# Attention of layer 1: row sums joined on VectorE, maxima spread by one product, and a fixed order on GpSimd

## The chip, the cores and the metric

The kernel runs on one core of one Trainium2 chip. The metric is the device time of one execution, in microseconds. Three executions were timed, and the median counts. One more execution was recorded by the profiler, and every duration of a single instruction below comes from that one.

## What is computed

The reference is a two-layer transformer in float32 over 1024 latent tokens and 256 context tokens of width 1024. Layer 1 mixes tokens by grouped-query attention: 16 query heads share 4 key and value heads of width 64, and each query sees all 1280 keys. Cut to this part it is

```
q = rms_norm(q, q_g); k = rms_norm(k, k_g); q, k = rope(q), rope(k)   # k of the context without rope
s = einsum('bqhgd,bkhd->bhgqk', q, k) * 64 ** -0.5                    # keys: 1024 latent, 256 context
p = softmax(s, axis=-1)
y = einsum('bhgqk,bkhd->bqhgd', p, v) @ w_out
h = h + gate * rms_norm(y, g_post)
```

A gated MLP with a width-3 convolution follows in both layers. The kernel computes its up and down projections by Strassen-like products of halves, for which sums and differences of blocks of the down projection's weights are made ahead of time.

## The kernel before

The attention of layer 1 is `odd_attn`. It walks over 32 blocks; a block is 128 queries of one key head, so four query heads and a tile of 128 x 512 scores per group of 128 keys. Ten such groups of keys make up the 1280. One block goes through these steps, each a small function:

- `maxima` (L1619), once per head: three TensorE products (L1622) give the scores of 128 queries against all 1280 keys in a tile of three PSUM banks, and VectorE takes the negated maximum of each row (L1623). The pool has one such tile, so the products of one head wait until the reduction of the head before has read it.
- `rounded` (L1625) and `shift` (L1629): ScalarE rounds the four columns of negated maxima to the fp32r format (L1627). Then four TensorE products of 128 columns each (L1633), every one with a broadcast column against the identity, turn these columns into rows that are the same on all partitions. ScalarE copies them (L1634) into the second operand of the scores, so that the score product subtracts the maximum by itself.
- `scores` (L1636), once per group of keys: two products of 512 columns (L1642) and an exponential on ScalarE (L1643) into `pT`.
- `values` (L1649): the products of the weights with the values (L1654), in two calls of five groups of keys.
- `first` (L1662) and `second` (L1669): the row sums. GpSimd adds the first eight tiles of `pT` into `part`, seven additions of 128 x 512 (L1667). VectorE adds the last two into `acc` (L1671).
- `sums` (L1656): TensorE multiplies a matrix of ones with `part` and then with `acc` (L1659), in the same PSUM accumulation, which gives the sums over all keys.
- `result` (L1673): VectorE takes the reciprocal (L1675) and multiplies (L1677), and two transfers store the block (L1680).

The blocks overlap. Iteration `n` of the loop holds the scores of block `n`, the second half of the values and `second` of block `n-1`, the sums and the result of block `n-2`, and the maxima of blocks `n+1` and `n+2`. The context manager `in_order` (L1683) keeps TensorE, VectorE and ScalarE in the order in which this loop is written. GpSimd is not listed there: its order, and that of the SyncE queue which issues the transfers, is chosen by the scheduler of the framework from a model of time, as everything outside such a bracket is.

Alongside runs `down_sums` (L609), a generator that prepares the weight sums of the down projection. For each of 11 slices it issues two loads (L618), gives way, makes two subtractions on GpSimd (L613), gives way, makes two more, gives way, issues the store (L628) and gives way. It has one buffer, so the next load waits for the store. The attention loop calls it by `self.steps(ts, 1 + n % 2)` (L1705) at the head of each iteration, one step in even and two in odd iterations. Layer 0 runs a generator of the same kind for its own weights, one step at a time from several loops, without a fixed order on GpSimd.

In iterations 29 to 32 the loop also loads the finished attention of the first 512 tokens and splits it into two operands for the output projection (`out_load`, L1742): ScalarE makes one half and GpSimd the other (L120). The output projection (products L317 to L319) starts right after the loop.

Of the kernel before, what the change touches and what calls it, by code (L numbers as in the profile page):

```python
# [10 lines left out]
F32R = mybir.dt.float32r  # L11
AF = mybir.ActivationFunctionType
ALU = mybir.AluOpType
# [4 lines left out]
P = 128  # L18
# [37 lines left out]
class Net:  # L56
# [92 lines left out]
    def constants(self):  # L149
        nc, a = self.nc, self.a  # L150
        c = lambda shape, tag, dt=F32: self.t(self.cst, shape, tag, None, dt)
        ld = nc.scalar.dma_start
        cv = c([P, KD, 2], "cv")
        ld(cv, a["c_cols"])
        self.ident = c([P, P], "ident")
        ld(self.ident, a["k_ident"])
        self.identr = c([P, P], "identr", F32R)
        nc.vector.tensor_copy(self.identr, self.ident)
        self.mhalf = c([P, 16], "mhalf")
        nc.vector.memset(self.mhalf, -0.5)  # L160
        self.ones = c([P, 64], "ones")
        nc.vector.memset(self.ones, 1.0)
        self.mone = c([P, 1], "mone")
        nc.vector.memset(self.mone, -1.0)
        self.cs = c([P, KD, 32], "cs")
        nc.vector.memset(self.cs, 0.0)
        nc.scalar.activation(self.cs[:, :, 0:2], cv, AF.Silu)
        self.bada = c([P, 2, 48], "bada")
        self.gateD = {}
        self.ada = [c([P, 48, 2], f"ada{l}") for l in range(2)]  # L170
        ld(self.bada, a["b_ada_cols"])
        self.ng = c([P, 2, 4, KD], "ng")
        ld(self.ng, a["norm_g_cols"])
        self.sel = c([P, 2], "sel")
        nc.vector.tensor_tensor(self.sel, self.ident[:, 0:2], self.ident[:, 32:34], op=ALU.add)
        for g in (2, 3):
            nc.vector.tensor_tensor(self.sel, self.sel, self.ident[:, 32 * g:32 * g + 2], op=ALU.add)
# [431 lines left out]
    def down_sums(self, l, pool):  # L609

        nc, w = self.nc, self.a["w_down"][l]
        self.tD[l] = [self.t(self.dr, [P, 2, D], f"tD{l}_{k}") for k in range(NH // 2)]
        sub = lambda o, x, y: nc.gpsimd.tensor_tensor(o, x, y, op=ALU.subtract)  # L613
        for k in range(NH // 2):
            r = self.t(pool(), [P, 2, D], "ts", 1)
            for h in range(2):
                i = k + h * (NH // 2)
                self.tc.keep_in_program_order(nc.sync.dma_start(r[:, h], w[i * P:(i + 1) * P, :]))  # L618
            yield

            (x, y), (u, v) = ((r[:, h, :HF], r[:, h, HF:]) for h in range(2))
            sub(y, y, x)
            sub(v, v, y)
            yield
            sub(x, v, x)
            sub(u, v, u)
            yield
            self.tc.keep_in_program_order(nc.sync.dma_start(self.tD[l][k], r))  # L628
            yield

# [970 lines left out]
    def odd_attn(self, es):  # L1601
        nc, tc = self.nc, self.tc
        with tc.tile_pool(name="ga", reuse_waits="tile", bufs=2) as gp, self.banks(two=1, turn=3, out=2):
            blocks = [dict(p=p, g=g, q=q) for p in range(4) for g in range(4) for q in range(2)]
# [14 lines left out]
            def maxima(b, h):  # L1619
                ps = self.t(self.b2, [P, 1536], "b2")  # L1620
                for c, w in ((0, 512), (512, 512), (T, C)):
                    nc.tensor.matmul(ps[:, c:c + w], b["q1"][:, h], self.KV[b["g"]][0][:, c:c + w], start=True, stop=True)  # L1622
                nc.vector.tensor_reduce(b["ng"][:, h:h + 1], ps[:, :S], axis=AX.X, op=ALU.max, negate=True)  # L1623

            def rounded(b):  # L1625
                b["mr"] = self.t(gp, [P, 4], "mr", 2, F32R)
                nc.scalar.copy(b["mr"], b["ng"])  # L1627

            def shift(b):  # L1629

                ps = self.t(self.bt, [P, 512], "b1")
                for h in range(4):
                    nc.tensor.matmul(ps[:, h * P:(h + 1) * P], b["mr"][:, h:h + 1].to_broadcast([P, P]), self.identr, start=True, stop=True)  # L1633
                nc.scalar.copy(b["q2"][64:P], ps[64:P].rearrange("p (h q) -> p h q", h=4))  # L1634

            def scores(b, k):  # L1636
# [9 lines left out]
            two = lambda x, i: x.rearrange("p (a b q) -> p a b q", a=2, b=2)[:, :, i]  # L1646
            out = lambda x, i: x[i * 64:i * 64 + 64].rearrange("p (a q) -> p a q", a=2)

            def values(b, k0, k1):  # L1649
                if k0 == 0:  # L1650
                    b["po"] = self.t(self.by, [P, 512], "by")
                for k in range(k0, k1):
                    for i in range(2):
                        nc.tensor.matmul(out(b["po"][:, :256], i), self.KV[b["g"]][2][:, k], two(b["pT"][:, k], i), start=(k == 0), stop=(k == NT - 1))  # L1654

            def sums(b):  # L1656
                for x in (b["part"], b["acc"]):
                    for i in range(2):
                        nc.tensor.matmul(out(b["po"][:, 256:], i), self.ones, two(x, i), start=(x is b["part"]), stop=(x is b["acc"]))  # L1659


            def first(b, k0, k1):  # L1662
                if k0 == 0:
                    b["part"] = self.t(gp, [P, 512], "part", 3)
                x = b["part"]
                for k in range(max(1, k0), k1):
                    nc.gpsimd.tensor_tensor(x, x if k > 1 else b["pT"][:, 0], b["pT"][:, k], op=ALU.add)  # L1667

            def second(b):  # L1669
                b["acc"] = self.t(gp, [P, 512], "acc", 3)  # L1670
                nc.vector.tensor_tensor(b["acc"], b["pT"][:, NT - 2], b["pT"][:, NT - 1], op=ALU.add)  # L1671

            def result(b):  # L1673
                rb = self.t(gp, [P, 256], "rb", 2)
                nc.vector.reciprocal(rb, b["po"][:, 256:])  # L1675
                ya = self.t(gp, [P, 256], "ya", 4)
                nc.vector.tensor_tensor(ya, b["po"][:, :256], rb, op=ALU.mult)  # L1677
                c0 = (2 * b["p"] + b["q"]) * P
                for i in range(2):
                    nc.sync.dma_start(self.yT1[2 * b["g"] + i][:, c0:c0 + P], ya[:, i * P:(i + 1) * P])  # L1680

            pinned = ExitStack()
            pinned.enter_context(self.in_order(nc.tensor, nc.vector, nc.scalar))  # L1683
            xp, ts = None, self.down_sums(1, lambda: gp)
            begin(blocks[0])
            begin(blocks[1])
            self.load_keys(gp, 2)
            for h in range(4):
                maxima(blocks[0], h)
            rounded(blocks[0])  # L1690
            for h in range(2):
                maxima(blocks[1], h)
            shift(blocks[0])
            for n in range(len(blocks) + 2):
                b, b1, b2, last, last2 = was(n), was(n + 1), was(n + 2), was(n - 1), was(n - 2)
                if n == 0:
                    self.load_keys(gp, 3)
                if b2:
                    begin(b2)
                if n == 29:  # L1700

                    self.es_g.close()
                    xp = es.enter_context(tc.tile_pool(name="xq", reuse_waits="tile", bufs=1, side="right"))
                    xm = self.xm_tiles(xp)
                self.steps(ts, 1 + n % 2)  # L1705
                if b:
                    scores(b, 0)
                if last2:
                    sums(last2)
                if last:  # L1710
                    values(last, 5, NT)
                if last2:
                    result(last2)
                if b1:
                    maxima(b1, 2)
                if b:
                    for k in (1, 2, 3, 4):
                        scores(b, k)
                    first(b, 0, 5)
                if b1:  # L1720
                    maxima(b1, 3)
                if b:
                    scores(b, 5)
                if b1:
                    rounded(b1)
                if last:
                    second(last)
                if b:
                    values(b, 0, 5)
                if b1:  # L1730
                    shift(b1)
                if b2:
                    maxima(b2, 0)
                if b:
                    for k in (6, 7, 8, 9):
                        scores(b, k)
                    first(b, 5, NT - 2)
                if b2:
                    maxima(b2, 1)
                if 29 <= n < 33:  # L1740
                    for k in (2 * (n - 29), 2 * (n - 29) + 1):
                        self.out_load(xm, k, self.yT1, 0, HF, self.t(gp, [P, 512], "raw", 2), "sp")  # L1742
# [104 lines left out]
```

## Time and profile before

| what | value |
|---|---|
| median of three executions | 2987.95 us |
| lowest and highest | 2986.34 and 2994.62 us |
| profiled execution, its own time | 2988.05 us |
| span of that execution | 2986.3 us |
| mean granted TensorE clock | 0.981 |
| TensorE busy | 2860.5 us, 96% |
| VectorE busy | 2082.2 us, 70% |
| GpSimd busy | 1595.6 us, 53% |
| ScalarE busy | 1295.4 us, 43% |

In the rows further down PE is TensorE's products, PEld its weight loads, DVE is VectorE, ACT is ScalarE, POOL is GpSimd and SP is SyncE. A number such as L1654 is a line of the kernel. A timeline row gives the start and the length in us, the engine, the line, the operation with its output and input tiles, and how many instructions were merged into the row; in square brackets stands the idle time before it and what ended that. A row of groups gives the shapes, the count, the busy time in us, the mean ns of one and the idle time before them.

### The profile page before, as it was taken

Reading aid. Unit: us, or ns where it says so; the run is one execution under the profiler, and the core shown is the slowest. Engines: PE = TensorE matmul, PEld = TensorE weight load, DVE = VectorE, ACT = ScalarE, POOL = GpSimd, SP = SyncE. Lnnn points to the kernel's source line nnn. Section 1 sums busy time; section 2 is a strip of 40 time slices with the busy share of each in tenths; the row PEclk is TensorE's granted clock in tenths of the full one; section 3 lists DMA queues with packets and bytes.
Section 4 is the critical chain, followed back from the end, with each engine's and each line's share of the span. In section 5 each row is a group of like instructions: output and inputs, shape, how many; then the busy total and the mean of one; then the engine's idle time right before and its main releaser. Section 6 shows DMA issues by size and latency. Waiting matters only on the chain.

```text
span 2986.3 us, 43134 instructions
## 1 busy us (share of the span) xinstructions
PE 2860.5 (96%) x15923; PEld 2280.3 (76%) x15923; DVE 2082.2 (70%) x2565; ACT 1295.4 (43%) x2255; POOL 1595.6 (53%) x1500
## 2 busy tenths in 40 slices
PE   8999999998999999999989989999998999999997
PEld 6868877776888888877769966666676788887785
DVE  4441255569776676788987666666647988887998
ACT  4221166473333333444466544444445344444443
POOL 2232268346333333265666778888855644442767
PEclk9999999999999999999999989999999999999999
DMA  9376664552323323543154553323252222225442
GB/s 319 112 239 203 216 238 154 187 185 94 111 91 125 120 97 120 195 162 127 57 188 122 153 165 109 105 90 99 73 175 85 80 86 82 81 82 193 163 141 85
DMA packets 234163, 411.29 MB, mean 138 GB/s; under 512 B 28240, under 2 KB 132688, under 8 KB 226016
## 3 DMA queue, kind: packets, MB, share of 16 engines
q1 hardware_dynamic: 211248, 392.99, 39.1%
q10 hardware_dynamic: 22704, 15.55, 1.7%
q8 instruction: 125, 2.05, 0.3%
q14 instruction: 86, 0.70, 0.1%
HBM read 303.54 MB, written 104.92 MB: 137 GB/s over the span
## 4 chain that ended last, share of the span: by engine, by line
PE 72%; DVE 10%; POOL 6%; DMA 4%; issue 4%; ACT 3%; ACTq 1%; SPq 0%; DVEq 0%; POOLq 0%
PE by L498 8%; PE by L500 8%; PE by L499 8%; PE b L1642 5%; PE by L1654 5%; PE b L1622 3%; PE by L873 3%; PE by L871 3%; PE by L872 3%; PE b L310 2%; PE b L306 2%; PE b L308 2%; DVE wlo L122 2%; PE by L318 2%; PE by L319 2%
## 5 line engine op out<-in xcount | busy, mean ns | idle before, releaser
L461 POOL TENSOR_TENSOR sw<-wraw,wraw 128x512 f32<-128x512 f32 x44 | 59.8, 1358 | 464.4 <-DVE wlo L122 464.4
L1623 DVE TENSOR_REDUCE ng<-b 128x1 f32<-128x1280 f32 x128 | 190.9, 1491 | 139.1 <-PE b L1622 139.1
L122 DVE TENSOR_TENSOR wlo<-wraw,whi 128x1024 fp32r<-128x1024 f32 (+1 forms) x160 | 213.7, 1341 | 87.4 <-ACT whi L116 87.3
L1667 POOL TENSOR_TENSOR part<-part,pT 128x512 f32<-128x512 f32 x192 | 253.6, 1321 | 13.3
L116 ACT CAST whi<-wraw 128x1024 fp32r<-128x1024 f32 (+1 forms) x160 | 157.8, 990 | 205.4 <-PE b L308 104.6
L1643 ACT ACTIVATE pT<-b 128x512 f32<-128x512 f32 x320 | 170.8, 602 | 157.9 <-PE b L1642 145.3
L116 ACT CAST whi<-sw 128x1024 fp32r<-128x1024 f32 x88 | 92.3, 1049 | 334.3 <-PE by L499 245.7
L498 PE MATMUL by<-xb,whi 128*128 128x512 f32 x528 | 212.1, 402 | 6.7 <-DVE xb L118 4.9
L499 PE MATMUL by<-xb,whi 128*128 128x512 f32 x528 | 210.4, 398 | 3.2 <-DVE xb L122 3.2
L500 PE MATMUL by<-xb,wlo 128*128 128x512 f32 x528 | 210.0, 398 | 3.0 <-DVE wlo L122 3.0
L477 DVE TENSOR_TENSOR z<-by,z 128x512 f32<-128x512 f32 x176 | 120.6, 686 | 131.5 <-POOL z L477 83.6
L613 POOL TENSOR_TENSOR ts<-ts 128x512 f32<-128x512 f32 x88 | 118.1, 1350 | 155.8 <-DMA ts<-in_w_down_dram 147.6
L122 DVE TENSOR_TENSOR xb<-xb,xb 128x512 fp32r<-128x512 f32 (+2 forms) x184 | 171.5, 947 | 23.0 <-ACT xb L116 22.2
L116 ACT CAST xb<-xb 128x512 fp32r<-128x512 f32 (+2 forms) x184 | 103.3, 567 | 180.6 <-PE by L872 62.7
L122 DVE TENSOR_TENSOR wlo<-sw,whi 128x1024 fp32r<-128x1024 f32 x88 | 129.2, 1468 | 65.3 <-ACT whi L116 64.7
L734 POOL TENSOR_TENSOR y<-y,wraw 128x512 f32<-128x512 f32 x72 | 113.7, 1600 | 88.1 <-DVE wraw L734 53.6
L1654 PE MATMUL by<-pT,Vs 128*64 128x256 f32 x1280 | 150.7, 382 | 0.0
L498 PE MATMUL by<-xm,whi 128*128 128x512 f32 x352 | 142.0, 403 | 8.9 <-DVE z L477 4.9
L516 DVE SCALAR_TENSOR_TENSOR o<-z,cw,o 128x1023 f32<-128x1023 f32 x88 | 141.4, 1609 | 0.9 <-ACT o L515 0.7
L498 PE MATMUL by<-xd,whi 128*128 128x512 f32 x352 | 139.7, 397 | 1.5 <-DVE xd L118 1.1
L499 PE MATMUL by<-xm,whi 128*128 128x512 f32 x352 | 140.9, 400 | 0.0
L500 PE MATMUL by<-xm,wlo 128*128 128x512 f32 x352 | 140.5, 400 | 0.0
(310 smaller groups left out, 8991.7 us busy)
## 6 DMA issues: line engine op xcount, KB each, us to landing
wraw<-in_w_up_t_dram SPq DMA_DIRECT2D x89, 512.0 KB
awr<-in_w_ada_dram SPq DMA_DIRECT2D x44, 1024.0 KB
ts<-in_w_down_dram SPq DMA_DIRECT2D x44, 512.0 KB
tD<-ts SPq DMA_DIRECT2D x22, 1024.0 KB
xm<-tD SPq DMA_DIRECT2D x88, 256.0 KB
hid<-o SPq DMA_DIRECT2D x43, 512.0 KB
xm<-in_w_down_dram SPq DMA_DIRECT2D x66, 256.0 KB
xb<-hid SPq DMA_DIRECT2D x66, 256.0 KB
```

The source lines that it names most:

```text
L116: nc.scalar.copy(hi, src)
L122: nc.vector.tensor_tensor(lo, src, hi.bitcast(F32), op=ALU.subtract)
L477: add = lambda o, x, y, e=V: e.tensor_tensor(o, x, y, op=ALU.add)
L498: nc.tensor.matmul(o, W[0][:, k, :], hi[k], start=(k == 0), stop=False)
L499: nc.tensor.matmul(o, W[0][:, k, :], lo[k], start=False, stop=False)
L500: nc.tensor.matmul(o, W[1][:, k, :], hi[k], start=False, stop=(k == 3))
L516: V.scalar_tensor_tensor(o[:, 1:], z[:, :n - 1], cw(0), o[:, 1:], op0=ALU.mult, op1=ALU.add)
L1623: nc.vector.tensor_reduce(b["ng"][:, h:h + 1], ps[:, :S], axis=AX.X, op=ALU.max, negate=True)
L1642: nc.tensor.matmul(ps.rearrange("p (h q) -> p h q", h=4), self.KV[b["g"]][i][:, c], b[f"q{i + 1}"], start=(i == 0), stop=(i == 1))
L1643: nc.scalar.activation(b["pT"][:, k], ps, AF.Exp)
L1654: nc.tensor.matmul(out(b["po"][:, :256], i), self.KV[b["g"]][2][:, k], two(b["pT"][:, k], i), start=(k == 0), stop=(k == NT - 1))
L1667: nc.gpsimd.tensor_tensor(x, x if k > 1 else b["pT"][:, 0], b["pT"][:, k], op=ALU.add)
```

## The change

The matrix of ones gets a sibling `onesr` of 128 x 128 in fp32r. Where ScalarE rounded four columns in one instruction, it now makes four diagonal matrices, each the identity scaled by one head's negated maxima, and one product of `onesr` with all four (512 columns) takes the place of four products of 128 columns. VectorE adds `part` to `acc`, so that `sums` has one operand instead of two. GpSimd joins the engines with a fixed order. The generator no longer gives way between its last subtractions and the store, so that a slice takes three steps instead of four, in both layers. In the attention it is called once per iteration, after the first GpSimd additions of the block, instead of once or twice at the head.

```diff
+        self.onesr = c([P, P], "onesr", F32R)
+        nc.vector.tensor_scalar(self.onesr, self.ident, 0.0, 1.0, op0=ALU.mult, op1=ALU.add)
...
             sub(x, v, x)
             sub(u, v, u)
-            yield
             self.tc.keep_in_program_order(nc.sync.dma_start(self.tD[l][k], r))
             yield
...
-            def rounded(b):
-                b["mr"] = self.t(gp, [P, 4], "mr", 2, F32R)
-                nc.scalar.copy(b["mr"], b["ng"])
+            def spread(b):
+
+                b["dm"] = self.t(gp, [P, 4, P], "dm", 2, F32R)
+                for h in range(4):
+                    nc.scalar.activation(b["dm"][:, h], self.ident, AF.Copy, scale=b["ng"][:, h:h + 1])
...
-                for h in range(4):
-                    nc.tensor.matmul(ps[:, h * P:(h + 1) * P], b["mr"][:, h:h + 1].to_broadcast([P, P]), self.identr, start=True, stop=True)
+                nc.tensor.matmul(ps.rearrange("p (h q) -> p h q", h=4), self.onesr, b["dm"], start=True, stop=True)
...
             def sums(b):
-                for x in (b["part"], b["acc"]):
-                    for i in range(2):
-                        nc.tensor.matmul(out(b["po"][:, 256:], i), self.ones, two(x, i), start=(x is b["part"]), stop=(x is b["acc"]))
+                for i in range(2):
+                    nc.tensor.matmul(out(b["po"][:, 256:], i), self.ones, two(b["acc"], i), start=True, stop=True)
...
                 nc.vector.tensor_tensor(b["acc"], b["pT"][:, NT - 2], b["pT"][:, NT - 1], op=ALU.add)
+                nc.vector.tensor_tensor(b["acc"], b["acc"], b["part"], op=ALU.add)
...
-            pinned.enter_context(self.in_order(nc.tensor, nc.vector, nc.scalar))
+            pinned.enter_context(self.in_order(nc.tensor, nc.vector, nc.scalar, nc.gpsimd))
...
-                self.steps(ts, 1 + n % 2)
...
                     first(b, 0, 5)
+                self.steps(ts, 1)
                 if b1:
                     maxima(b1, 3)
                 if b:
                     scores(b, 5)
                 if b1:
-                    rounded(b1)
+                    spread(b1)
                 if last:
                     second(last)
```

## Rows read from the trace of the kernel before

**Rows 1.** The page: TensorE's busy time, and the chain that ended last.
```profile
PE 2860.5 (96%) x15923; PEld 2280.3 (76%) x15923; DVE 2082.2 (70%) x2565; ACT 1295.4 (43%) x2255; POOL 1595.6 (53%) x1500
...
PE 72%; DVE 10%; POOL 6%; DMA 4%; issue 4%; ACT 3%; ACTq 1%; SPq 0%; DVEq 0%; POOLq 0%
```

**Rows 2.** Windows: two blocks of layer 1's attention, busy us of each engine, clock, transfers.
```profile
1922.00:1949.00 27.00, 27.00 (x171) 18.33 (x170) 17.93 (x15) 12.51 (x26) 20.69 (x17) 1.00 0.35 118
```

**Rows 3.** Timeline of TensorE, one block and the ends of its neighbours.
```profile
1937.61 2.33 PE L1654 MATMUL by<-pT,Vs 128*64 128x256 f32 x20
...
1940.78 0.39 PE L1642 MATMUL b<-q,k 128*128 128x512 f32 x1
1941.01 0.39 PE L1642 MATMUL b<-Q,k 128*128 128x512 f32 x1
...
1943.59 2.38 PE L1654 MATMUL by<-pT,Vs 128*64 128x256 f32 x20
1945.89 0.66 PE L1633 MATMUL b<-identr,mr 128*128 128x128 f32 x4
1946.39 0.79 PE L1622 MATMUL b<-k,Q 128*128 128x512 f32 x3
...
1948.91 0.74 PE L1622 MATMUL b<-k,Q 128*128 128x512 f32 x3
...
1950.53 0.60 PE L1659 MATMUL by<-acc,ones 128*64 128x256 f32 x4
1950.96 2.33 PE L1654 MATMUL by<-pT,Vs 128*64 128x256 f32 x20
```

**Rows 4.** Timeline of ScalarE in the same block.
```profile
1941.21 2.07 ACT L1643 ACTIVATE pT<-b 128x512 f32<-128x512 f32 x4 [3.77 <-PE b L1642]
1943.69 0.60 ACT L1643 ACTIVATE pT<-b 128x512 f32<-128x512 f32 x1 [0.41 <-PE b L1642]
1944.75 0.19 ACT L1627 CAST mr<-ng 128x4 fp32r<-128x4 f32 x1 [0.46 <-DVE ng L1623]
```

**Rows 5.** Groups by line and shape on ScalarE, whole span: the nearest to a scaled diagonal.
```profile
L378 ACT ACTIVATE xd<-b,ada,A 128x256 f32<-128x256 f32 x64 | 31.2, 565 | 4.5 <-PE b L374 4.4
...
L1500 ACT COPY xb<-by 128x256 f32<-128x256 f32 x42 | 15.7, 374 | 11.7 <-PE by L319 9.1 <-POOL xb L1511 2.4
...
L1363 ACT COPY rb<-b 128x128 f32<-128x128 f32 x40 | 10.8, 271 | 3.0 <-PE b L1335 3.0
```

**Rows 6.** Timeline of VectorE in the same block.
```profile
1943.23 1.49 DVE L1623 TENSOR_REDUCE ng<-b 128x1 f32<-128x1280 f32 x1 [0.99 <-PE b L1622]
1944.63 1.12 DVE L1671 TENSOR_TENSOR acc<-pT 128x512 f32<-128x512 f32 x1
1947.22 1.49 DVE L1623 TENSOR_REDUCE ng<-b 128x1 f32<-128x1280 f32 x1 [1.47 <-PE b L1622]
```

**Rows 7.** Instructions of line L1671: ns min/median/max; then its group with its mean.
```profile
L1671 DVE TENSOR_TENSOR acc<-pT x32: 679/786/1799, 1771.1 to 2175.9; 128x512 f32<-128x512 f32 x32
...
L1671 DVE TENSOR_TENSOR acc<-pT 128x512 f32<-128x512 f32 x32 | 33.3, 1040 | 0.0
```

**Rows 8.** Timeline of GpSimd around the same VectorE addition, and into the next block.
```profile
1945.16 1.72 POOL L1667 TENSOR_TENSOR part<-pT 128x512 f32<-128x512 f32 x1
1946.96 8.11 POOL L1667 TENSOR_TENSOR part<-part,pT 128x512 f32<-128x512 f32 x6
1955.25 1.30 POOL L1667 TENSOR_TENSOR part<-pT 128x512 f32<-128x512 f32 x1 [0.17 <-ACT pT L1643]
```

**Rows 9.** Groups on GpSimd, 1733 to 2185 us, the stage of layer 1's attention.
```profile
L1667 POOL TENSOR_TENSOR part<-part,pT 128x512 f32<-128x512 f32 x192 | 253.6, 1321 | 13.3
L613 POOL TENSOR_TENSOR ts<-ts 128x512 f32<-128x512 f32 x44 | 58.3, 1333 | 32.2 <-DMA ts<-in_w_down_dram 25.1 <-DMA yU<-ya 4.5 <-ACT mr L1627 1.8
```

**Rows 10.** Timelines at the end of the stage: GpSimd's last L613 and last L120, TensorE's first L317.
```profile
2120.00 1.29 POOL L613 TENSOR_TENSOR ts<-ts 128x512 f32<-128x512 f32 x1
...
2182.20 1.29 POOL L120 TENSOR_TENSOR xm<-raw,xm 128x512 fp32r<-128x512 f32 x1 [0.81 <-ACT xm L116]
...
2175.84 0.49 PE L317 MATMUL by<-whi,xm 128*128 128x512 f32 x1
```

More of the change, by code (lines that the diff above doesn't have):

```diff
@@ L1689, in odd_attn @@
                 maxima(blocks[0], h)
-            rounded(blocks[0])
+            spread(blocks[0])
             for h in range(2):
```

## The prediction

> **What bounds the kernel now.** I read the page first. TensorE is busy for 96% of the span, and 72% of the chain that ended last is its products [rows 1]. So time is saved only where TensorE has less to do or waits less. Next come the windows over the stage that the change touches: in 27 us TensorE is busy for all 27.00 at granted clock 1.00, its 2.4 GHz level, while VectorE has 17.93 and GpSimd 20.69 [rows 2]. The stage has no idle TensorE to win back; what counts is the length of its own list, and whether another engine becomes longer. Then the timeline of one block. The second half of the values starts at 1937.61 and again at 1950.96, so a block takes 13.35 us [rows 3]. There are 32 blocks. Last I read, engine by engine, how long before its reader each changed step is done.
>
> The sums below are made against the profiled execution's own time, 2988.05 us, which is 0.1 us from the median of 2987.95. A measurement of this kernel can tell about 0.3%, 9 us, from no change.
>
> **Row sums: TensorE's part.** The products of ones with `acc` occupy TensorE from 1950.53 to 1950.96, 0.43 us [rows 3]. They go, and the values behind them move up. The products with the joined sum remain at the old price of the first pair. Gain 0.43 x 32 = 13.8 us.
>
> **Maxima to rows: TensorE's part.** The four short products hold TensorE from 1945.89 to 1946.39, 0.50 us, though they have 512 columns together [rows 3]. Two products of 512 columns in the same format start 0.23 us apart (1940.78 and 1941.01) [rows 3]. The new one is of that kind, so 0.23 us is the low end of its price; the high end is the old 0.50. I take 0.25, near the low end, with 0.02 for changing from the values' shape: gain 0.25 x 32 = 8.0 us. Both gains together are 0.68 us of 13.35 per block, 21.8 us in all.
>
> **Maxima to rows: ScalarE's part.** One 0.19 us instruction becomes four. No row shows a 128 x 128 scaled copy from SBUF. The floor is that of the small cast, 0.19 us each [rows 4]; the ceiling is 0.57, a 128 x 256 instruction with two vectors as operands [rows 5]. A plain 128 x 128 copy took 0.27, and two vector operands cost 565 - 374 = 191 ns on 256 columns, so about 0.1 each [rows 5]: 0.37 for one alone. Four exponentials back to back took 2.07 where one takes 0.60, so each after the first costs 0.49, 0.11 less [rows 4]. Four diagonals then take 0.37 + 3 x 0.26 = 1.15 us. If all four wait for the fourth maximum, they start at 1944.75, where the cast starts now [rows 4], and end at 1945.90; TensorE wants them at 1945.89 [rows 3]. If the first three run as soon as the exponential before them ends, at 1944.29, the last ends earlier. So this fits with nothing to spare: 0 to 0.05 us of waiting, and 1.1 us in the worst corner (four times 0.57 from 1944.75, ending at 1947.03). I take 1 us for the whole stage. What queues behind on ScalarE is the copy of the rows and the next exponentials; the copy waits for the product anyway.
>
> **Row sums: VectorE's part.** Its second addition stands between the reduction that ends at 1944.72 and the one that starts at 1947.22 [rows 6]. With the shorter product that next reduction can start at 1946.97. It frees the only three-bank tile, which TensorE wants for the next head at 1948.91, 0.20 us after the reduction's end at 1948.71 [rows 3, 6]. From 1944.63 the two additions thus have 2.34 us before they delay the reduction, and 2.54 before they delay TensorE. One addition takes 0.68 at best, 1.04 on average and 1.80 at worst [rows 7]. Two take 1.36, 2.08 or 3.60; the average fits and the worst overruns by 1.06. The spread comes from GpSimd: the 1.12 us one starts at 1944.63, GpSimd finishes an addition at 1945.16, VectorE's ends at 1945.75, and the GpSimd addition beside it takes 1.72 where 1.29 to 1.32 is usual [rows 6, 8, 9]. I take the mean, and for its spread 0.25 us in one block of four, 2 us in all. The bounds are 0 and 1.06 x 32 = 34 us.
>
> The Trainium skill, "SBUF — State Buffer", section "SBUF: two separate sides", has a rule that speaks against this part: VectorE with two SBUF inputs and GpSimd share one port pair, and whichever starts first keeps it for its whole instruction. The row of 1.72 us agrees; taken strictly, each addition would meet a running GpSimd instruction most of the time, and the worst case would be the usual one, which the 0.79 us median in that row group doesn't bear out for one addition. That case is the second rival.
>
> The new addition also waits for `part`. Behind that wait stand the next reductions and so TensorE. GpSimd ends a block's additions as the next block's second exponential comes out (1955.25, after 0.17 us of idling) [rows 8], and VectorE's addition comes 2.7 us behind that point (1957.98 by the 13.35 us step). With two subtractions put in between, GpSimd has 7 x 1.32 + 2 x 1.33 = 11.9 us of work in a block of 12.67, in two blocks of three [rows 9]. It keeps up, and `part` costs nothing until GpSimd is over 2.7 us late.
>
> **The steps of the weight sums.** There are 33 of them now for 34 iterations, where 44 steps ended at 2120 [rows 10]. Each load gets an iteration to land, so the 25.1 us that GpSimd waited for loads [rows 9] should mostly go; nobody on the path was waiting for it. The store now sits in SyncE's queue while the subtractions run, with the next block's loads behind it for at most a couple of us; those have most of an iteration to land. I count both as nothing. In layer 0 the 11 stores move up in the same way, past weight loads; TensorE has weights ahead there, and I count nothing, with 3 us either way for the range as a choice, not a row.
>
> The end of the stage is different. GpSimd's last subtraction used to be done four blocks before the end, and its last operand for the output projection came at 2182.20, 6.4 us after the projection's first product [rows 10]. Now three pairs of subtractions, 6 x 1.33 = 8.0 us [rows 9], fall into iterations 29, 31 and 32, in written order ahead of those operands. GpSimd was all but full there. The projection can begin with the operands it has, on up to four tiles, which covers part. Bounds 0 and 8 us; I take 3.
>
> Sum: -13.8 - 8.0 + 1 + 2 + 3 = -15.8 us. After the stage TensorE is again the bound, so an earlier start carries to the end. 2988.05 - 15.8 = 2972.3; forecast 2972, with an own range of 2965 to 2979.
>
> **The rivals.**
>
> *GpSimd's written order starves the end.* The last operands come 8 us later and the output projection stands still for them. For it: GpSimd's fullness and the fixed order, which cannot pull the operands forward. Against it: TensorE had other products to place there. The gain shrinks by 5 to 9 us more: 2977 to 2981, taken as 2981. Chance 0.14.
>
> *VectorE's pair becomes the bound; slower.* If the second addition regularly waits for a GpSimd instruction as well as the first, the pair takes 3.60 us, the reduction is late by 1.26 and TensorE stands still 1.06 us per block. From 0.68 us of standing still per block, so a pair of 3.2 us, the gain is gone. 34 - 21.8 + 1 + 3 = +16: 3004. For it: the 1.80 us row. Against it: the median is 0.79 and GpSimd's additions start from the same exponential in each block, so the meeting point repeats. Chance 0.08.
>
> *The single product isn't what it seems.* If it takes the pace of the values' products (ten of 256 columns, two instructions each, from 1943.59 to 1945.89, so 0.46 us for 512 columns [rows 3]), nothing is left of 8.0 us: 2980. Both operands are declared fp32r like the scores', so I give it 0.03.
>
> *Stages outside move.* The order there comes from a model of time, and a shift of 15 us or a missing pause can change it in either direction by some us. Chance 0.15 that it covers the forecast's own range by more: 0.08 further down (2960 to 2965), 0.05 to about no change, 0.02 slower.
>
> **How the numbers follow.** Forecast 0.60, rivals 0.14, 0.08, 0.03, 0.15. Faster than 2979 holds the forecast and the downward part of the last: 0.68. Within 0.3% hold the first and third rival and 0.05: 0.22. Slower: 0.10. The likeliest case gives 2972. The range runs from 2961, where all bounds are kind (21.8 + 0.6 for a product of 0.23, and 3 from layer 0, with little else, give 2963), to 2992, above the first and third rivals; what it leaves out is chiefly the VectorE case.
>
> **What would show it.** Block spacing on TensorE's timeline of 12.7 instead of 13.35 us; about 0.5 us for the sums and 0.25 to 0.35 for the single product; four ScalarE instructions that end at or before the product's start; VectorE's pair under 2.3 us and no TensorE wait for L1623's reduction. Wrong would be a wait of TensorE for that reduction in most blocks, GpSimd additions ending after VectorE asks for them, or an idle TensorE at the start of L317's products.

## The result and the profile after

The changed kernel takes 2974.33 us (median of 6 runs, 2968.9 to 2977.39); the kernel before, on the same occasions, 2994.72 (6 runs, 2986.34 to 2998.53). The ratio is 0.9936, 95% interval 0.9922 to 0.995: faster by 20.4 us by the medians. Between the two profiled executions the gain is 15.5 us (2988.05 and 2972.55; spans 2986.3 and 2970.8).

The page, engines' busy time, against [rows 1]; then the same window as [rows 2], busy us of PE, PEld, DVE, ACT and POOL, then granted clock, transfers' share and GB/s:

```profile
PE 2844.2 (96%) x15699; PEld 2265.2 (76%) x15699; DVE 2115.3 (71%) x2598; ACT 1326.0 (45%) x2351; POOL 1611.4 (54%) x1500
```

```profile
1922.00:1949.00 27.00, 27.00 (x162) 18.12 (x161) 21.88 (x17) 15.36 (x33) 25.07 (x19) 1.00 0.24 83
```

TensorE lost 16.3 us of work, about the gain of the span, and in these blocks is as full as before at the same granted clock (1.00, the 2.4 GHz level). VectorE went from 17.93 to 21.88 us in 27, GpSimd from 20.69 to 25.07.

TensorE's timeline of one block, against [rows 3]:

```profile
1931.47 2.33 PE L1656 MATMUL by<-pT,Vs 128*64 128x256 f32 x20
...
1937.44 2.38 PE L1656 MATMUL by<-pT,Vs 128*64 128x256 f32 x20
1939.75 0.50 PE L1635 MATMUL b<-dm,onesr 128*128 128x512 f32 x1
1940.08 0.75 PE L1623 MATMUL b<-k,Q 128*128 128x512 f32 x3
...
1943.68 0.65 PE L1660 MATMUL by<-acc,ones 128*64 128x256 f32 x4
1944.16 2.33 PE L1656 MATMUL by<-pT,Vs 128*64 128x256 f32 x20
...
1956.16 0.86 PE L1623 MATMUL b<-k,Q 128*128 128x512 f32 x3 [0.72 <-DVE ng L1624]
```

In the trace before, the sums start with this row:

```profile
1950.05 0.65 PE L1659 MATMUL by<-part,ones 128*64 128x256 f32 x4
```

From start to start, the sums take 0.48 us where two pairs took 0.91 (1950.05 to 1950.96), and the single product 0.33 where four took 0.50. The second half of the values starts at 1931.47 and at 1944.16, 12.69 us later instead of 13.35. The last row of the changed kernel is what is new on the bad side: in the block that follows, TensorE stands still 0.72 us for VectorE's reduction.

The span can be followed through one mark per block, the start of VectorE's reciprocal of the sums (L1675 before, L1677 after):

| stretch | before | after | difference |
|---|---|---|---|
| start to the first reciprocal | 1777.68 | 1778.48 | +0.8 |
| the next 28 gaps | 373.68 | 358.88 | -14.8 |
| the last three gaps | 33.27 | 34.95 | +1.7 |
| last reciprocal to last L317 (after: L319) product | 90.2 | 88.3 | -1.9 |
| from there to the end | 711.5 | 710.2 | -1.3 |

A usual gap went from 13.35 to 12.71 us. In 28 gaps that would be 17.9 us; three gaps of 13.7 (one is the block above) give 3.0 back. The last gap is 13.91 where it was 10.83. These two losses are what the experiments look into.

### The profile page after: what moved, and what is told of

It reads as the page before. It is cut to its first block, busy times and chain, and to the rows that moved or that the text cites. A ratio compares the mean times of both kernels' runs of the same rounds, so it can differ in the third digit from the quotient of the medians.

```text
span 2970.8 us, 42877 instructions
## 1 busy us (share of the span) xinstructions
PE 2844.2 (96%) x15699; PEld 2265.2 (76%) x15699; DVE 2115.3 (71%) x2598; ACT 1326.0 (45%) x2351; POOL 1611.4 (54%) x1500
## 5 line engine op out<-in xcount | busy, mean ns | idle before, releaser
L1668 POOL TENSOR_TENSOR part<-part,pT 128x512 f32<-128x512 f32 x192 | 271.3, 1413 | 13.4
L502 PE MATMUL by<-xd,wlo 128*128 128x512 f32 x352 | 138.7, 394 | 0.0
```

Of the source, the lines that this page charges most:

```text
L502: nc.tensor.matmul(o, W[1][:, k, :], hi[k], start=False, stop=(k == 3))
```

## The experiments

Each kernel is timed beside the kernel before on the same chip; "spacing" is the gap between reciprocals.

**The row sums alone** (e1): the kernel before, with the second VectorE addition and one operand for the sums. GpSimd's order isn't fixed and a slice has four steps.

```diff
                 nc.vector.tensor_tensor(b["acc"], b["pT"][:, NT - 2], b["pT"][:, NT - 1], op=ALU.add)
+                nc.vector.tensor_tensor(b["acc"], b["acc"], b["part"], op=ALU.add)
...
-                for x in (b["part"], b["acc"]):
-                    for i in range(2):
...
+                for i in range(2):
+                    nc.tensor.matmul(out(b["po"][:, 256:], i), self.ones, two(b["acc"], i), start=True, stop=True)
```

> The kernel before with only the second VectorE addition and the halved sums; GpSimd stays unpinned and the weight sums keep their four steps. Theory: TensorE loses 0.43 us per block (0.91 to 0.48 us for the sums), 13.8 us in 32 blocks, but GpSimd's old order runs subtractions ahead of the additions, so that part is late in a few blocks and VectorE's second addition waits for it; I expect 3 to 8 us of that back, net -6 to -11 us, and waits of VectorE's new line for GpSimd in the trace. Rival: the fixed order on GpSimd does nothing, part is always early enough, net -11 to -14 us and no such waits.

Measured: 2978.45 against 2992.53, ratio 0.9951 (0.9935 to 0.9967), 14.1 us. The usual spacing is 12.91, so the sums give 0.44 us a block. But nine of the first 28 gaps are over 13, up to 13.79. VectorE's timeline in one of those:

```profile
1904.53 1.67 DVE L1670 TENSOR_TENSOR acc<-pT 128x512 f32<-128x512 f32 x1
1906.30 1.60 DVE L1671 TENSOR_TENSOR acc<-acc,part 128x512 f32<-128x512 f32 x1
1907.83 1.48 DVE L1623 TENSOR_REDUCE ng<-b 128x1 f32<-128x1280 f32 x1
```

The pair takes 3.3 us, with no wait before the second addition: what lengthens this block is the duration of both, not a late `part`. In seven more of the nine it is the same, with a first addition of 1.18 to 1.78 us. In the ninth, the longest, the second addition waits 1.17 us for `part`. In the whole stage `part` is waited for 4 times, 8.5 us, the longest 4.9. The 28 gaps are 4.1 us longer than 28 usual ones (365.6 for 361.5), so the loss that the theory expected is there, for the most part by another cause; going by the time alone, the rival would look right.

**The maxima by one product alone** (e2): the kernel before with `onesr`, the diagonals and the single product.

```diff
-                b["mr"] = self.t(gp, [P, 4], "mr", 2, F32R)
-                nc.scalar.copy(b["mr"], b["ng"])
+                b["dm"] = self.t(gp, [P, 4, P], "dm", 2, F32R)
+                for h in range(4):
+                    nc.scalar.activation(b["dm"][:, h], self.ident, AF.Copy, scale=b["ng"][:, h:h + 1])
...
-                for h in range(4):
-                    nc.tensor.matmul(ps[:, h * P:(h + 1) * P], b["mr"][:, h:h + 1].to_broadcast([P, P]), self.identr, start=True, stop=True)
+                nc.tensor.matmul(ps.rearrange("p (h q) -> p h q", h=4), self.onesr, b["dm"], start=True, stop=True)
```

> The kernel before with only the four diagonals and their single product; the rest as before. Theory: the product takes 0.33 us of TensorE instead of 0.50 and the maxima behind it start 0.04 us better, 0.21 us per block, 6.7 us in all; the diagonals end before TensorE asks for them, so nothing is given back: -5 to -8 us, block spacing 13.14 us. Rival: the diagonals are late where TensorE does not have the longer list of the changed kernel around them, and ScalarE's wait eats it: -2 to +3 us.

Measured: 2982.98 against 2992.53, ratio 0.9968 (0.9955 to 0.9981), 9.6 us. The spacing is 13.11 to 13.17 in all 28 gaps: 0.21 us a block, 6.7 us in 32. TensorE's timeline:

```profile
1941.97 0.50 PE L1635 MATMUL b<-dm,onesr 128*128 128x512 f32 x1
1942.31 0.74 PE L1624 MATMUL b<-k,Q 128*128 128x512 f32 x3
```

The product holds TensorE for 0.34 us here, so this size comes from the product itself and not from what the sums do beside it.

**GpSimd without a fixed order** (e3): the changed kernel, one word less.

```diff
-            pinned.enter_context(self.in_order(nc.tensor, nc.vector, nc.scalar, nc.gpsimd))
+            pinned.enter_context(self.in_order(nc.tensor, nc.vector, nc.scalar))
```

> The changed kernel with GpSimd taken out of the fixed order, nothing else. Theory: the scheduler's order places subtractions ahead of additions, part comes after VectorE's second addition asks for it in some blocks, and TensorE stands still for the reduction behind it: 5 to 20 us slower than the changed kernel, so -12 to +3 us against the kernel before. Rival: the fixed order is worth nothing; within 3 us of the changed kernel, about -16 us.

Measured: 2982.46 against 2992.53, ratio 0.9967 (0.9957 to 0.9977): some 8 us slower than the changed kernel, whose interval lies wholly lower. Eleven of the first 28 gaps are 13.3 to 14.1, and the last but one is 16.46. GpSimd's timeline before one of the long blocks, then VectorE's and the weight load's (PEld) in it:

```profile
2003.46 1.28 POOL L615 TENSOR_TENSOR ts<-ts 128x512 f32<-128x512 f32 x1 [0.66 <-ACT dm L1630]
2004.69 1.74 POOL L1668 TENSOR_TENSOR part<-part,pT 128x512 f32<-128x512 f32 x1
2006.39 1.29 POOL L615 TENSOR_TENSOR ts<-ts 128x512 f32<-128x512 f32 x1
...
2015.20 7.41 POOL L1668 TENSOR_TENSOR part<-part,pT 128x512 f32<-128x512 f32 x5
```

```profile
2015.58 1.45 DVE L1672 TENSOR_TENSOR acc<-pT 128x512 f32<-128x512 f32 x1
2017.13 1.60 DVE L1673 TENSOR_TENSOR acc<-acc,part 128x512 f32<-128x512 f32 x1
```

```profile
2020.19 0.53 PEld L1623 LDWEIGHTS b<-k,Q 128*128 128x128 f32 x3 [0.83 <-DVE ng L1624]
```

Subtractions are put between the additions one by one, and shift those of the next block against VectorE. Its first addition then starts 0.38 us after one of GpSimd's, takes 1.45 instead of 0.68, and the reduction is late. `part` is waited for three times, 16.2 us in all: 1.2 in the first block, which is in the gap of 14.1, then 9.9 and 5.1 in the last two. Against the changed kernel the 28 gaps are 5.8 us longer together (364.6 and 358.9; 3.7 against the 361.0 of its second trace, e11).

The end of the stage makes up for that. Windows from the 29th reciprocal to the last L319 product of the projection, the changed kernel's and then e3's, length first and TensorE's busy us behind it:

```profile
2137.36:2260.59 123.23, 118.51 (x568) 90.02 (x565) 69.46 (x72) 62.29 (x126) 75.34 (x78) 0.99 0.50 175
...
2151.60:2268.99 117.39, 116.92 (x568) 89.13 (x565) 67.62 (x72) 61.53 (x122) 72.39 (x77) 1.00 0.50 171
```

TensorE idles 4.7 us there in the changed kernel and 0.5 in e3. From the first reciprocal to that product both take the same, 482.1 us (482.9 in e11) and 482.0. So the times show that the fixed order is worth some 8 us, and the traces show that it makes the blocks shorter and the end longer; where the 8 us come from they don't show. This execution of e3 starts the attention 4.1 us later, takes 4.4 more from there to the first reciprocal and 6.6 more behind the projection, and is near the slow end of its nine (2987.51; 2978.07 to 2987.94).

**The old steps with the order fixed** (e9): the changed kernel with the four steps per slice, taken once or twice at the head of each iteration as before.

```diff
             sub(u, v, u)
+            yield
...
+                self.steps(ts, 1 + n % 2)
...
-                self.steps(ts, 1)
```

> The changed kernel, GpSimd in the fixed order, but the weight sums in four steps, called once or twice at the head of the iteration as before. Theory: in a fixed order a subtraction that follows its load in the same iteration holds GpSimd up for the transfer (about 4 us), and four subtractions in one iteration overfill it; part is then late for VectorE's second addition in every third or fourth block, each costing 1 to 3 us: 6 to 20 us slower than the changed kernel. Rival: 2.7 us of room for part absorbs it, within 3 us.

Measured: 2977.76 against 2993.29, ratio 0.9944 (0.9929 to 0.9959). The expected loss didn't come. The spacing is 12.71 but for 13.05 and 13.26, and from the first product of the maxima to the last of the projection it takes 520.2 us where the changed kernel takes 524.2. Waits in the stage, in us, times, longest; then GpSimd's timeline with four subtractions in one place:

```profile
POOL ts L615 <- DMA ts<-in_w_down_dram: 7.4, 5, 1.9
...
DVE acc L1674 <- POOL part L1669: 2.6, 1, 2.6
```

```profile
1774.75 5.27 POOL L615 TENSOR_TENSOR ts<-ts 128x512 f32<-128x512 f32 x4
1779.97 1.28 POOL L1669 TENSOR_TENSOR part<-pT 128x512 f32<-128x512 f32 x1
```

Loads are waited for, and four subtractions hold the additions up by 5.3 us, yet `part` is late only once, at the end. Changing the steps is worth no time that shows. In the traces the old steps even have the shorter stage: the last subtraction is done at 2123.80 (2174.66 in the changed kernel), the last gap is 10.17 (13.91 in the changed kernel), and from the first reciprocal to the last projection product it takes 476.6 us, where the changed kernel takes 482.1. The late end of the changed kernel came with the new steps.

**VectorE's pair taken apart** (e5): the changed kernel with the first addition one reduction earlier, `pair(last)` right after `maxima(b1, 2)`.

```diff
+            def pair(b):
+                b["acc"] = self.t(gp, [P, 512], "acc", 3)
+                nc.vector.tensor_tensor(b["acc"], b["pT"][:, NT - 2], b["pT"][:, NT - 1], op=ALU.add)
...
                     maxima(b1, 2)
+                if last:
+                    pair(last)
```

> The changed kernel with VectorE's first addition moved ahead, behind the reduction of the third head's maxima, where VectorE idles 0.97 us; the second addition stays alone behind the fourth's. Theory: in the changed kernel three blocks take 13.7 instead of 12.7 us because the first addition meets a running GpSimd addition (1.80 us) and the second again (1.59 us), 3.5 us in one gap of 2.5 us; alone, each fits even at its worst. No block of 13.7 us is left, spacing 12.71 us throughout, the attention 3 us shorter than in the changed kernel. Rival: moving it only moves the waiting, to the fourth head's maxima or the diagonals that need them: spacing rises by 0.2 to 0.7 us in many blocks, 5 to 20 us slower.

Measured: 2974.33 against 2993.29, ratio 0.9931 (0.9914 to 0.9947), equal to the changed kernel. All 28 gaps are 12.69 to 12.76: no long block is left. VectorE's timeline:

```profile
1941.59 1.57 DVE L1672 TENSOR_TENSOR acc<-pT 128x512 f32<-128x512 f32 x1
1943.09 1.48 DVE L1624 TENSOR_REDUCE ng<-b 128x1 f32<-128x1280 f32 x1
1944.49 1.71 DVE L1675 TENSOR_TENSOR acc<-acc,part 128x512 f32<-128x512 f32 x1
```

Now both additions meet GpSimd (1.5 and 1.7 us on average), and it costs no block anything, since either has a gap of its own. The total was never the trouble; two long ones in a row were.

**A third addition** (e6), behind the pair, into a tile that nothing reads.

```diff
                 nc.vector.tensor_tensor(b["acc"], b["acc"], b["part"], op=ALU.add)
+                b["jk"] = self.t(gp, [P, 512], "jk", 2)
+                nc.vector.tensor_tensor(b["jk"], b["acc"], b["part"], op=ALU.add)
```

> The changed kernel with a third VectorE addition of the same size behind the second, into a tile that nobody reads. Theory: the gap between the fourth head's reduction and the next block's first one is used up (VectorE's rows stand back to back there in the changed kernel), TensorE is 0.1 to 0.2 us from waiting, so a third addition of 0.68 to 1.8 us goes to the block's length nearly whole: 0.6 to 1.6 us per block, 20 to 50 us slower than the changed kernel, and TensorE waits for the reduction in every block. Rival: VectorE still has slack, 24% of its time idle in the stage, and it costs under 5 us.

Measured: 3024.36 against 2993.29, ratio 1.0098 (1.0081 to 1.0115). VectorE's timeline, then TensorE's:

```profile
1955.39 0.68 DVE L1672 TENSOR_TENSOR acc<-pT 128x512 f32<-128x512 f32 x1
1956.17 1.58 DVE L1673 TENSOR_TENSOR acc<-acc,part 128x512 f32<-128x512 f32 x1
1957.79 1.67 DVE L1675 TENSOR_TENSOR jk<-acc,part 128x512 f32<-128x512 f32 x1
```

```profile
1960.91 0.85 PE L1623 MATMUL b<-k,Q 128*128 128x512 f32 x3 [1.30 <-DVE ng L1624]
```

The spacing is 14.27, 1.56 us more, in nearly all blocks. VectorE's place is that tight: additions that take 4.1 us from the first's start to the last's end (1955.39 to 1959.46), where the pair takes 2.4, make a slower kernel than before. The slower rival's mechanism is real; in the change it just doesn't happen often.

**An earlier end of the weight sums** (e7): four iterations take two steps.

```diff
-                self.steps(ts, 1)
+                self.steps(ts, 2 if n in (2, 7, 12, 17) else 1)
```

> The changed kernel with two steps of the weight sums instead of one in iterations 2, 7, 12 and 17, so that they end with iteration 28 and none falls into the last four. Theory: GpSimd's last addition of the last block comes 2.6 us earlier and its last operand for the output projection 5 us earlier, VectorE's wait of 7.8 us for part in the last block shrinks, and the stage with the first products of the output projection gets 1 to 4 us shorter. Rival: TensorE fills that time with other products anyway (it is busy for all but 5 us of 2150 to 2200 us), and the end moves by less than 1 us.

Measured: 2974.30 against 2993.29, ratio 0.9937 (0.9922 to 0.9952); by its time, nothing. The trace shows the place, though. VectorE's wait for `part` in the stage:

```profile
DVE acc L1673 <- POOL part L1668: 2.6, 1, 2.6
```

The changed kernel has 10.3 us there. The last gap falls from 13.91 to 10.17; from the first reciprocal to the projection's last product it takes 478.8 instead of 482.1, of which 1.0 is one block of 13.7 less (two for three).

**A pause in layer 0** (e4): in the changed kernel, layer 1's attention started 3.4 us later than before (first product of its maxima at 1736.4 and 1733.0). To see whether the earlier stores of layer 0 do it, that layer gets its pause back.

```diff
             sub(u, v, u)
+            if l == 0:
+                yield
```

> The changed kernel with the removed pause put back in layer 0 only. Theory: the three steps per slice in layer 0 make its loads denser where transfers are at 0.74 to 0.85 of the engines, and TensorE's waits for the loads of w_ada (3.0 us in three waits, absent before) come from that; with the pause back they go, and TensorE idles about 1 us instead of 4.6 in 200 to 250 us; layer 1's attention starts 2 to 4 us earlier: 2 to 4 us under the changed kernel. Rival: these waits are the transfers' usual spread and stay, or go without moving the start of the attention: within 1 us.

Measured: 2976.08 against 2992.53, ratio 0.9944 (0.9927 to 0.9962). The attention starts at 1743.1, later still, and TensorE waits for a `w_ada` load here as well, once for 2.6 us (three times, 3.0 us, in the changed kernel):

```profile
PE bx L197 <- DMA awr<-in_w_ada_dram: 2.6, 1, 2.6
```

That theory falls. The six kernels e3, e5, e6, e7, e10 and e11 have the changed kernel's lines ahead of the stage and start at 1740.5, 1738.2, 1742.6, 1736.4, 1733.9 and 1735.5: a spread of 9 us that no edit there explains. The changed kernel lies in it; the kernel before lies 0.9 us under its low end, and e1 and e2, with the old steps there, start at 1735.9 and 1733.3. No part of the change is shown to move the start.

**Both weak places mended** (e10, the edits of e5 and e7 together), beside **the changed kernel once more** (e11), five executions each.

> The changed kernel with both edits that shortened the stage in a trace: VectorE's first addition moved behind the third head's reduction, and the weight sums ended by iteration 28. Theory: no block of 13.7 us (3 us) and an earlier end of the stage (2.5 us), so 2 to 6 us under the changed kernel beside it on the same chip, about -22 to -25 us against the kernel before. Rival: both gains are within what executions of one kernel differ by (8 us between the lowest and the highest), and the medians are within 2 us.

> The changed kernel itself once more, unedited, as the yardstick for the run beside it and for where its start of layer 1's attention falls in another execution. Theory: layer 0's later start of 3.4 us is the spread between executions, so its trace puts the first L1623 anywhere from 1733 to 1744 us; -17 to -21 us against the kernel before. Rival: it comes from the change, and the start lies at 1736 to 1737 us again.

Measured against 2994.73: e10 2970.67 us, ratio 0.9926 (0.9912 to 0.9939); e11 2973.92, ratio 0.9932 (0.992 to 0.9945). All 28 gaps of e10 are 12.68 to 12.73 and the last is 10.17; e11 has five gaps of 13.7 where the first profile had three (and e4 one, with the same attention). From first reciprocal to last projection product: 476.5 and 482.9 us. That is 6.3 us less of the stage; the medians differ by 3.3, and the intervals overlap, so the lead is seen in the trace and isn't settled by the times.

## Why the prediction was right

It forecast 2972 us, 15.8 less than before; the profiled executions differ by 15.5, the medians of the common occasions by 20.4. The range and the sign held. That the forecast lies only 2 us from the measured 2974.33 is partly luck: the gain in the medians is 4.6 us larger than forecast, and the three executions before that it started from have a median 6.8 us under that of all six. Inside the sum two small errors nearly cancel: TensorE's own gain is 1.3 us smaller than counted (0.64 us a block, 20.5 for 21.8), and the 1 us for ScalarE wasn't needed. Its steps:

**What bounds the stage: right.** TensorE is full before and after, but for 2.2 us in the three long blocks, and the gain of the span is the work taken from it. e6 shows how near VectorE is to being the bound.

**Row sums on TensorE: right.** -0.43 us a block was counted; 0.91 became 0.48, and e1 alone gave 0.44.

**The single product: mechanism right, term too kind.** 0.25 us was taken, the 0.23 of two such products in a row and 0.02 for changing from the values' shape; measured 0.33. So the term for the change was too small, and the trace before had its price: the three products of the maxima stand there behind the values as well as behind scores.

```profile
1939.86 0.85 PE L1622 MATMUL b<-k,Q 128*128 128x512 f32 x3
1940.55 0.40 PE L1642 MATMUL b<-Q,k 128*128 128x512 f32 x1
...
1942.43 0.76 PE L1622 MATMUL b<-k,Q 128*128 128x512 f32 x3
1943.03 0.39 PE L1642 MATMUL b<-Q,k 128*128 128x512 f32 x1
```

From start to start they take 0.69 us behind the values and 0.60 behind scores (0.68 and 0.58 in the median of the stage). That is 0.1 us for entering the group behind the values, and 0.23 with 0.1 is the 0.33 measured. The weight load in front of the single product also stands idle for as long as it did in front of the four, 11.9 us in 31 blocks (the waits of L1635 and of L1633). So one product carries alone what four shared; what causes it, no run tests. The maxima behind it take 0.59 where they took 0.63, so that e2 has 0.21 us a block of the 0.25 counted. With the sums that makes 0.64 for 0.68.

**Diagonals on ScalarE: right, and the corner didn't occur.** The timeline against [rows 4], and the group:

```profile
1938.04 1.26 ACT L1630 ACTIVATE dm<-ident,ng 128x128 fp32r<-128x128 f32 x4
```

```profile
L1630 ACT ACTIVATE dm<-ident,ng 128x128 fp32r<-128x128 f32 x128 | 40.7, 391 | 2.1 <-DVE ng L1624 2.1
```

One takes 391 ns in the mean (0.37 us estimated), four together 1.26 us (1.15). They start at 1938.04, before the fourth reduction ends at 1938.57, because the first three have their maxima; they end at 1939.30, 0.45 us before the product. The microsecond counted for waiting was not needed.

**VectorE's pair: size about right (3.0 us for 2), reason incomplete.** It takes 2.36 us in a usual block, just over the 2.3 named as the mark, and the other sign, no TensorE wait for the reduction, failed in three blocks. VectorE's timeline in a usual block and in a long one:

```profile
1937.08 1.49 DVE L1624 TENSOR_REDUCE ng<-b 128x1 f32<-128x1280 f32 x1 [0.97 <-PE b L1623]
1938.49 0.68 DVE L1672 TENSOR_TENSOR acc<-pT 128x512 f32<-128x512 f32 x1
1939.27 1.58 DVE L1673 TENSOR_TENSOR acc<-acc,part 128x512 f32<-128x512 f32 x1
...
1951.20 1.80 DVE L1672 TENSOR_TENSOR acc<-pT 128x512 f32<-128x512 f32 x1
1953.11 1.59 DVE L1673 TENSOR_TENSOR acc<-acc,part 128x512 f32<-128x512 f32 x1
1954.62 1.48 DVE L1624 TENSOR_REDUCE ng<-b 128x1 f32<-128x1280 f32 x1
```

The same moments on GpSimd's timeline (instructions one by one):

```profile
1938.55 1.75 POOL L1668 TENSOR_TENSOR part<-part,pT 128x512 f32<-128x512 f32 x1
...
1951.18 1.27 POOL L1668 TENSOR_TENSOR part<-part,pT 128x512 f32<-128x512 f32 x1
1952.53 1.62 POOL L1668 TENSOR_TENSOR part<-part,pT 128x512 f32<-128x512 f32 x1
```

At 1938.49 VectorE starts 0.06 us ahead of GpSimd: it takes 0.68, and GpSimd 1.75 instead of 1.27. At 1951.20 it starts 0.02 us behind: it takes 1.80, GpSimd 1.27. The second addition meets the next GpSimd one both times. Three VectorE additions that waited end 0.55 us after the GpSimd one beside them (1952.45 to 1953.00, 1954.15 to 1954.70, 1940.30 to 1940.85). The rule that the prediction drew from the Trainium skill, "SBUF — State Buffer", section "SBUF: two separate sides", agrees with these rows: the one that starts first has its short duration (0.68 or 1.27 us), and the other goes on only when it is done. The prediction let it count as a spread of the mean of [rows 7]; in fact the second addition meets GpSimd in the usual block, and the first is decided by hundredths of a microsecond. In 29 of 32 blocks the two engines start within 0.09 us of each other. VectorE had the short duration in 26 of these. In the other three (gaps of 13.7) TensorE stood still.

**`part` late: right in the blocks, and the end.** The waits for it in the stage, and of TensorE for the reduction:

```profile
DVE acc L1673 <- POOL part L1668: 10.3, 2, 7.8
PE b L1623 <- DVE ng L1624: 9.1, 8, 2.1
```

All the waiting for `part` is in the last two blocks. For the reduction TensorE waited 6.4 us in 5 waits in the kernel before; the three new waits are those of the long blocks, 2.2 us. GpSimd's end of the stage, against [rows 10]:

```profile
2162.57 2.65 POOL L615 TENSOR_TENSOR ts<-ts 128x512 f32<-128x512 f32 x2
2165.19 4.03 POOL L1668 TENSOR_TENSOR part<-part,pT 128x512 f32<-128x512 f32 x3
2169.17 2.98 POOL L120 TENSOR_TENSOR xm<-raw,xm 128x512 fp32r<-128x512 f32 x2
2172.12 2.54 POOL L615 TENSOR_TENSOR ts<-ts 128x512 f32<-128x512 f32 x2
2174.62 2.52 POOL L120 TENSOR_TENSOR xm<-raw,xm 128x512 fp32r<-128x512 f32 x2
```

The subtractions stand ahead of the last additions and operands, as the prediction said. It counted 3 us. From first reciprocal to last projection product, after against e7 shows 2.3 (3.3 less the 1.0 of the extra long block), e11 against e7 1.1 (4.1 less 3.0 for three), and e5 against e10, which differ in this alone and have no long blocks, 4.5 (481.0 and 476.5), but with a granted clock of 0.97 against 1.00 behind the 29th reciprocal. TensorE's idle time from that reciprocal to the last product spreads less: 4.7 us in the changed kernel and in e11 and 5.2 in e5, against 2.65 in e7 and e10 and 3.4 in the kernel before. What it had not seen is that the last block's row sums are late too, not just the projection's operands.

**Steps and layer 0, counted at nothing: nothing shown against it.** e9 and e4 move the time by no more than the spread.

Of the rivals, the starved end did not grow beyond the forecast's 3 us or so. The slower one has its mechanism in 3 blocks (5 in e11) rather than in all. The product at half pace fell: 0.33, not 0.46. The written order of GpSimd, treated as a cost in a rival, was by the times a gain: e3 loses about 8 us without it, and the prediction had no term for that, since its sum took the old phase of GpSimd's additions as given. In the traces both sides are seen: with it the 28 gaps are 3.7 to 5.8 us shorter, and the stretch behind them is 4.5 to 5.8 us longer (121.9 in e11 and 123.2, against 117.4).

Open: why the medians differ by 5 us more than the profiled executions. The start of the stage spreads by 9 us between kernels that are alike up to there, which is enough to cover it; no run separates the two. Open too is what the 8 us of the fixed order are made of. Both edits without a fixed order and with the old steps were not run together: e1 and e2 gain 14.1 and 9.6 us that way by themselves, e3, which has both with the new steps, 10.1, so the loss of e3 may belong to the new steps in a free order rather than to the free order alone.

## What to carry to other kernels

When the bound engine is full, count its instructions from start to start at their place in the list: a lone product behind a group of another shape costs more than its pace in a row (0.33 against 0.23 us), and a group that already stands in such a place shows the price (0.1 us here). Before putting a second SBUF addition on VectorE beside a GpSimd that adds all the time, price each at the met duration (about 1.6 to 1.8 us here, not 0.68), and give each a gap of its own rather than one gap for both. An order fixed by hand is also a fixed phase between two engines; here it made the blocks 4 to 6 us shorter, and put work ahead of the end of the stage that cost about as much there.

## What was not expected of the hardware

Two engines' additions started within 0.09 us of each other in 29 of 32 blocks, and a lead of 0.02 us on GpSimd's side at 1951.18 went with 1.1 us more for VectorE (1.80 against 0.68) and a block longer by 1.0 us. The same kernel had three such blocks in one execution and five in another. In hundredths the lead doesn't tell who will win: VectorE also took 0.68 at 1836.82, with GpSimd's record at 1836.80. The records in the traces go to the nanosecond, and there it does, almost. In the changed kernel, e11, e4 and e7, among starts within 0.1 us of each other, VectorE took 0.68 wherever GpSimd's start is recorded later or up to 15 ns earlier than its own (13 ns at 1836.82), and 1.80 or 1.81 in all ten cases of 17 to 20 ns; at 16 ns three were short and one was long.
